# The shared expert's up projections ahead of the routing lists, and its result as the first content of the second sum

## Chip, cores and metric

One NeuronCore of a Trainium2 chip runs the whole kernel. The metric is device microseconds for one execution, median over runs. Engines: TensorE (PE, with its weight loads PEld), VectorE (DVE), ScalarE (ACT), GpSimd (POOL), SyncE (SP, which here only issues DMAs), and 16 DMA engines.

## What is computed

One layer of a decoder trunk over 512 tokens of width 1024: a conditioned norm, three token mixers, a gated residual, then a second conditioned norm and a mixture of experts (64 routed experts of width 256, top 8 of 4 groups; one shared expert), a gated residual and a last norm. The part around the change:

```python
scores = jax.nn.sigmoid(xt @ router_w)          # 512 x 64
...                                             # top 8 experts of each token, weights top_w
yb = (silu(xb @ w1[e]) * (xb @ w3[e])) @ w2[e] * wt    # each expert, on its tokens
routed = sum over experts, scattered to tokens
shared = (silu(xt @ sw1) * (xt @ sw3)) @ sw2    # all 512 tokens
x = x + g2 * (routed + shared)
return rmsnorm(x, final_norm)
```

## The kernel before

Tokens lie in four tiles of 128. The tail of the program, which the change touches, has five stages.

**Projections of the mixers** (from L738 on): weights are split into a high and a low part and multiplied in three passes. On ACT's queue two DMAs of 1 MB (L789) set the DRAM tensor `acc2`, the second of two sums over tokens, to zero from a zeroed tile `z0`; the first sum is `acc`, which gets x after the mixers (L956).

**Output projection and router**, tile by tile (L935 to L985). For each tile `t` the normalised rows `h2` are made on DVE, where POOL supplies the inverse root (`rsq`, L70, stored in `root[t]`); PE transposes them (L968) into `h2F[t]` and multiplies with the router (L973). `route(t)` on DVE finds each token's eight experts (the mask `Mb`, L884). `place(t)` counts positions by PE (L890, L891), then DVE makes eight table indices `ti` and eight rows `row`, one after the other. `fill(t)` has POOL write those eight columns into the DRAM table by eight indirect DMAs (L912): `fill(0)` is issued at tile 2, `fill(1)` and `fill(2)` at tile 3, `fill(3)` after the loop.

**Lists** (L1017 to L1083): from the counts of all tiles (`cps`, L1019) DVE makes `items`, the lists of expert runs, in some sixty small operations; PE turns two of them (L1081). The table is then read back as `idxw` and `idc` (L1098, L1104), and POOL gathers the first run's rows with it (L1120, L1127).

**Shared expert** (L1311 to L1332): for each tile 8 up matmuls in plain f32 (L1319, weights `shw`), silu and product (`act_a`, L1162, L1163), two transposes (L1323), 4 down matmuls (L1330), the gate (L1331) into `ysh[t]`. The scheduler places these instructions wherever an engine has nothing older to do. The results are added to `acc` by four indirect accumulating DMAs (`add_a`, L1191, indices `tok`, L1314).

**Routed experts**: a loop of runs (`pair_of_runs`, 16 of them here, then 9 single blocks). Before it, in an order written out by hand from L1338 on, come the gathers, the transposes of the gathered rows (`x_a`, L1146), copies of the gate row (L1349, L1352) and the splits of the first expert's weights (`split_a(0, u)`, six pieces `wh`, `wl`; ACT makes the high part at L49, DVE the low part at L50). `pair_of_runs` begins on PE with a transpose (L1202) and the up matmuls in three passes (L1153 to L1155).

Each engine takes its instructions in order, so what stands ahead on an engine delays what follows. SP issues the DMAs of expert weights in program order too.

Of the kernel before, what the change touches and what calls it, by code (L numbers as in the profile page):

```python
# [27 lines left out]
E = 64  # L28
# [6 lines left out]
def trunk(ctx, tc, x, c, ada_w, ada_b, norm1, norm2, w_in, conv_a_w, conv_a_b, ln_a_g, ln_a_b,  # L35
# [725 lines left out]
    for j in range(4):  # L761
# [8 lines left out]
        for h in range(2):  # L770
# [10 lines left out]
            for i in range(2):  # L781
                hi, lo = (mT[a][i][:, :, 2 * j + h] for a in range(2))
                A.activation(hi, mt[:, 2 * i:2 * i + 2], AF.Copy, scale=0.5)
                V.scalar_tensor_tensor(lo, mt[:, 2 * i:2 * i + 2], 0.5, hi.bitcast(F32), op0=OP.mult, op1=OP.subtract)
    z0 = mp.tile([P, 4 * E, 2], F32, name="z0")
    G.memset(z0, 0.0)
    a2v = acc2.rearrange("(g p) d -> p g d", p=P)
    for h in range(2):
        nc.scalar.dma_start(a2v[:, :, h * 512:h * 512 + 512],  # L789
                            z0.rearrange("p c x -> p (c x)")[:, None].to_broadcast([P, TT, 512]))  # L790
    tb = mp.tile([P, 4 * E, 2], F32, name="tb")
    G.memset(tb, 0.0)
    tb2 = tb.rearrange("p (c b) x -> p c b x", b=2)
# [142 lines left out]
    for ts in ((0, 1), (2,), (3,)):  # L936
# [7 lines left out]
        for t in ts:  # L944
# [36 lines left out]
                place(0, *sM[0][:2])  # L981
            if t > 1:
                with tc.issue_after(root[t].ins):
                    for v in (0,) if t == 2 else (1, 2):
                        fill(v)  # L985
            if t == 2:
                first_two()
# [26 lines left out]
    load_up(ra, None, 0)  # L1014
    load_down(rad[0], None, 0)

    cps = psh.tile([P, E], F32, name="ps_m", bufs=2)  # L1017
    for t in range(TT):
        T.matmul(cps, ones_b, Mb[:, t], start=(t == 0), stop=(t == TT - 1))  # L1019
# [58 lines left out]
    for a, src in enumerate((v_, c_)):  # L1078
        ips = psh.tile([1, 3, P], F32, name="it_ps", tag="ps_m", bufs=2)
        for j in range(3):  # L1080
            T.matmul(ips[:, j], src[:, j:j + 1], ident, start=True, stop=True)  # L1081
        V.tensor_copy(iv[:, a], ips)
    V.tensor_copy(items[:, 6, 0:2], mi[0:1, 1:3])  # L1083
    hst.close()
    rawst.close()
# [50 lines left out]
    def split_a(j, u, up=None):  # L1136
        if u < 4:
            src = (up or ra[j % 2]).rearrange("p (z k f) -> p k z f", z=2, k=KT)[:, 2 * u:2 * u + 2]
            split(*(w[u].rearrange("p (k z f) -> p k z f", k=2, z=2) for w in (wh, wl)), src)
        else:  # L1140
            split(wh[u], wl[u], rad[j % 2][:, (u - 4) * 1024:(u - 3) * 1024])
# [7 lines left out]
    def up_a(ph, u):  # L1149
        for k in (2 * u, 2 * u + 1):  # L1150
            q = slice(k % 2 * 512, k % 2 * 512 + 512)
            for b in ph:
                T.matmul(ph[b], h2T[0][b][:, k], wh[u][:, q], start=(k == 0), stop=False)  # L1153
                T.matmul(ph[b], h2T[0][b][:, k], wl[u][:, q], start=False, stop=False)  # L1154
                T.matmul(ph[b], h2T[1][b][:, k], wh[u][:, q], start=False, stop=(k == KT - 1))  # L1155

    def ps_up(bs):
        return {b: pse.tile([P, 512], F32, name="ph", bufs=2) for b in bs}

    def act_a(ph, w=None):  # L1160
        hw = ew.tile([P, 256], F32, name="hw", bufs=2)
        A.activation(hw, ph[:, :256], AF.Silu)  # L1162
        V.scalar_tensor_tensor(hw, hw, 1.0 if w is None else w.bitcast(F32), ph[:, 256:], op0=OP.mult, op1=OP.mult)  # L1163
        return hw

    def turn_a(hws):
        n = len(hws)
# [22 lines left out]
    def add_a(y, at, beside=None, to=acc):  # L1190
        st = G.indirect_dma_start(out=to, out_offset=IOA(ap=at, axis=0), in_=y, in_offset=None,  # L1191
                                  compute_op=OP.add, bounds_check=S - 1, oob_is_err=False)
        g = beside or f"run {st.ins.name}"
        if beside:
            tc.declare_no_dep(st.ins, group=g, reason="the rows of a run are distinct")
        tc.add_to_no_dep_group(g, st.ins)
        return g
# [110 lines left out]
        add_a(down_b(i, hT), sa[:, 0, 0:1], to=acc2)  # L1308
        load_down(rad[i % 2], GL, i + 2)

    gs, tok = rad[1][:, :D], ew.tile([P, TT], I32, name="tok")  # L1311
    nc.sync.dma_start(gs, modr[3:4].to_broadcast([P, D]))
    for t in range(TT):
        G.tensor_scalar(tok[:, t:t + 1], iop, 128.0 * t, None, op0=OP.add)  # L1314
    run, ysh = None, []
    for t in range(TT):
        ph = ps_up((t,))[t]
        for k in range(KT):
            T.matmul(ph, h2F[t][:, k], shw[k // 2][:, k % 2 * 512:k % 2 * 512 + 512], start=(k == 0), stop=(k == KT - 1))  # L1319
        hw = act_a(ph)  # L1320
        p3 = pse.tile([P, 2, 2, P], F32, name="p3")
        for k in range(2):
            T.transpose(p3[:, 0, k], hw[:, k * P:(k + 1) * P], ident)  # L1323
        hb = ew.tile([P, 2, P], F32, name="hb", tag="hh")
        A.activation(hb, p3[:, 0], AF.Copy)
        y = rc[1][:, t % 2 * D:t % 2 * D + D] if t > 1 else ew.tile([P, D], F32, name="y", bufs=2)
        for h in range(2):
            py, q = pse.tile([P, 512], F32, name="py", bufs=2), slice(h * 512, h * 512 + 512)
            for k in range(2):
                T.matmul(py, hb[:, k], shw[4 + k][:, q], start=(k == 0), stop=(k == 1))  # L1330
            V.tensor_tensor(y[:, q], py, gs[:, q], op=OP.mult)  # L1331
        ysh.append(y)  # L1332
    wh = [ew1.tile([P, 1024], F32R, name=f"wh{u}") for u in range(6)]
# [4 lines left out]
    with tc.manual_schedule():  # L1338
        gather_a(GA, 0)
        copied = gather_c(GC, 0)  # L1340
        for t in range(2):
            run = add_a(ysh[t], tok[:, t:t + 1], run)
        load_up(rc, GC, 0, copied)
        load_down(rcd, GC, 0)
        for g in range(4):
            x_a(g // 2, g % 2)
        gather_a(GA, 1)
        nc.sync.dma_start(fn[0:1], final_norm[None, :])
        A.activation(gm2, gs, AF.Copy)  # L1349
        for z in range(2):  # L1350
            zq = slice(z * CH, z * CH + CH)
            A.activation(gm2c[zq], gs[zq, z * 512:z * 512 + 512], AF.Copy)  # L1352
        for t in range(2, TT):
            run = add_a(ysh[t], tok[:, t:t + 1], run)
        for u in range(6):
            split_a(0, u)
        load_down(rad[1], GA, 1)
        with ExitStack() as nest:
            for i in range(15):
# [57 lines left out]
```

## Time and profile before

| | |
|---|---|
| time, median of 3 runs | 1458.77 us (1456.04 to 1461.76) |
| the profiled execution's own time | 1467.86 us |
| its span, first to last instruction | 1466.1 us |
| PE busy | 1347.5 us (92%) |
| DVE, ACT, POOL busy | 956.0, 620.3, 264.8 us |
| DMA | 289.13 MB, mean 197 GB/s |

The profile page gives busy time per engine and in 40 slices of the span. The views below it list one engine's instructions in order of time with the idle time before each and what ended it (timeline), the sums of such waits (waits), and the busy time of all engines in chosen stretches (windows). A plain f32 matmul stands as two records, so "x12" of L1319 are six matmuls. "PEclk" is the share of TensorE's full clock that was granted.

### The profile page before, as it was taken

The numbers are of one execution on the slowest core, as the hardware profiler recorded it, in microseconds if no ns is written. First come the engines' busy times: TensorE is split into PE (matmuls) and PEld (weight loads), VectorE is DVE, ScalarE is ACT, GpSimd is POOL, SyncE is SP. The second block draws the span as 40 slices with busy tenths as digits, with TensorE's granted clock in tenths as the row PEclk, the third lists the DMA queues.
The fourth block names the chain that finished last, engine by engine and source line by source line (L and its number), as shares of the span: only waits on it lengthen the run. The fifth ranks groups of instructions, "written<-read, shape, count | busy, mean of one in ns | idle before, by whom it ended". The sixth has DMA issues, their size and how long they took to land. (4 is left out here: it accounts for less than half of the span.)

```text
span 1466.1 us, 24089 instructions
## 1 busy us (share of the span) xinstructions
PE 1347.5 (92%) x8982; PEld 968.7 (66%) x8982; DVE 956.0 (65%) x1816; ACT 620.3 (42%) x1019; POOL 264.8 (18%) x255
## 2 busy tenths in 40 slices
PE   4999999999999979998998978999999999997881
PEld 3877777776766756664686635777677777774660
DVE  6865998987777777233455855666656566564664
ACT  4454334427568658220212213434434443443442
POOL 1000000000000000000000354243342524333332
PEclk8999999999999989999999989999999999999996
DMA  9321231232112117759826348999898989966985
GB/s 339 110 58 31 66 89 47 69 125 92 31 59 80 31 51 237 242 185 333 278 74 238 134 154 266 371 341 322 322 313 294 314 301 337 321 219 206 317 285 208
DMA packets 120634, 289.13 MB, mean 197 GB/s; under 512 B 14883, under 2 KB 68397, under 8 KB 109486
## 3 DMA queue, kind: packets, MB, share of 16 engines
q1 hardware_dynamic: 99266, 242.87, 46.2%
q0 software_dynamic: 17904, 36.01, 10.0%
q10 hardware_dynamic: 3324, 8.49, 1.6%
q8 instruction: 75, 1.23, 0.3%
q14 instruction: 65, 0.53, 0.1%
HBM read 260.24 MB, written 46.97 MB: 210 GB/s over the span
## 5 line engine op out<-in xcount | busy, mean ns | idle before, releaser
L53 PE MATMUL ps_in<-hT_hi,w_hi 128*128 128x512 f32 x496 | 203.9, 411 | 2.7 <-ACT hT_hi L49 2.7
L54 PE MATMUL ps_in<-hT_hi,w_lo 128*128 128x512 f32 x496 | 201.5, 406 | 0.3 <-DVE w_lo L50 0.2
L55 PE MATMUL ps_in<-hT_lo,w_hi 128*128 128x512 f32 x496 | 199.9, 406 | 0.0
L50 DVE TENSOR_TENSOR wl<-ra,wh 128x1024 fp32r<-128x1024 f32 x100 | 122.1, 1224 | 115.2 <-ACT wh L49 111.6
L49 ACT ACTIVATE wh<-ra 128x1024 fp32r<-128x1024 f32 x100 | 105.6, 1060 | 127.8 <-PE ph L1155 90.0
L1153 PE MATMUL ph<-wh,mT_hi 128*128 128x512 f32 x328 | 134.5, 410 | 2.3 <-ACT wh L49 2.3
L1154 PE MATMUL ph<-wl,mT_hi 128*128 128x512 f32 x328 | 129.6, 395 | 0.5 <-DVE wl L50 0.5
L1155 PE MATMUL ph<-wh,mT_lo 128*128 128x512 f32 x328 | 129.3, 394 | 0.0
L50 DVE TENSOR_TENSOR w_lo<-w_raw,w_hi 128x1024 fp32r<-128x1024 f32 x76 | 92.5, 1223 | 51.0 <-ACT w_hi L49 50.8
L53 PEld LDWEIGHTS ps_in<-hT_hi,w_hi 128*128 128x128 f32 x496 | 94.6, 191 | 34.3 <-issue 7.6
L1191 POOL DMA_INDIRECT acc<-y,sa x41 | 65.6, 1599 | 272.9 <-DVE hc L1227 238.0
L54 PEld LDWEIGHTS ps_in<-hT_hi,w_lo 128*128 128x128 f32 x496 | 94.4, 190 | 21.7 <-issue 1.7
L55 PEld LDWEIGHTS ps_in<-hT_lo,w_hi 128*128 128x128 f32 x496 | 94.3, 190 | 21.8 <-issue 2.7
L49 ACT ACTIVATE w_hi<-w_raw 128x1024 fp32r<-128x1024 f32 x76 | 79.3, 1052 | 38.8 <-PE ps_p L55 18.3
L594 DVE SCALAR_TENSOR_TENSOR u<-ut,par,u 128x512 f32<-128x512 f32 x120 | 84.2, 747 | 0.6
L70 POOL TENSOR_TENSOR h<-h,mhalf 128x4 f32<-128x4 f32 x8 | 10.5, 1310 | 358.4 <-DVE h L393 358.4
L1153 PEld LDWEIGHTS ph<-wh,mT_hi 128*128 128x128 f32 x328 | 62.7, 191 | 18.2 <-issue 3.4
L1154 PEld LDWEIGHTS ph<-wl,mT_hi 128*128 128x128 f32 x328 | 62.8, 191 | 15.3 <-issue 1.9
L1155 PEld LDWEIGHTS ph<-wh,mT_lo 128*128 128x128 f32 x328 | 62.6, 191 | 13.3
L1187 DVE TENSOR_TENSOR y<-py,rows 128x512 f32<-128x512 f32 x64 | 44.1, 689 | 31.9 <-PE py L1185 25.1
L49 ACT ACTIVATE wh<-rad 128x1024 fp32r<-128x1024 f32 x34 | 34.1, 1050 | 71.8 <-issue 36.1
L1120 POOL DMA_INDIRECT xg<-h2d,ia x45 | 56.3, 1250 | 20.3 <-issue 8.8
(523 smaller groups left out, 2754.5 us busy)
## 6 DMA issues: line engine op xcount, KB each, us to landing
ra<-in_exp_w_dram SPq DMA_DIRECT2D x52, 1024.0 KB
rc<-in_exp_w_dram SPq DMA_DIRECT2D x34, 1024.0 KB
w_raw<-in_w_in_dram SPq DMA_DIRECT2D x31, 1024.0 KB
rad<-in_exp_w_dram SPq DMA_DIRECT2D x27, 1024.0 KB
adar<-in_ada_w_dram SPq DMA_DIRECT2D x32, 512.0 KB
rcd<-in_exp_w_dram SPq DMA_DIRECT2D x16, 1024.0 KB
ada<-in_ada_w_dram SPq DMA_DIRECT2D x8, 1024.0 KB
gd<-sg SPq DMA_DIRECT2D x24, 256.0 KB
```

What stands on the lines that cost most here:

```text
L49: A.activation(hi, src, AF.Copy)
L50: (lo_engine or V).tensor_tensor(lo, src, hi.bitcast(F32), op=OP.subtract)
L53: T.matmul(ps, l[0], r[0], start=first, stop=False)
L54: T.matmul(ps, l[1], r[0], start=False, stop=False)
L55: T.matmul(ps, l[0], r[1], start=False, stop=last)
L594: V.scalar_tensor_tensor(u[:, ct], ut[ct][:, w:w + S], col("caw", w * 4 + ct), u[:, ct], op0=OP.mult, op1=OP.add)
L1120: G.indirect_dma_start(out=xg[b], out_offset=None, in_=h2d, in_offset=IOA(ap=ia[s][:, b, 0:1], axis=0), bounds_check=S - 1, oob_is_err=False)
L1153: T.matmul(ph[b], h2T[0][b][:, k], wh[u][:, q], start=(k == 0), stop=False)
L1154: T.matmul(ph[b], h2T[0][b][:, k], wl[u][:, q], start=False, stop=False)
L1155: T.matmul(ph[b], h2T[1][b][:, k], wh[u][:, q], start=False, stop=(k == KT - 1))
L1187: V.tensor_tensor(y[:, q], py, gate[:, q], op=OP.mult)
L1191: st = G.indirect_dma_start(out=to, out_offset=IOA(ap=at, axis=0), in_=y, in_offset=None, compute_op=OP.add, bounds_check=S - 1, oob_is_er ...
```

## The change

Five edits. The zeroing of `acc2` goes. The shared expert is split: its 32 up matmuls, the silu, the product and the transposes are written before the lists' counts, for all tiles (silu in `sil`, the linear half copied to `lin`, turned into `hb4`); the 16 down matmuls stay where they were. The four results are written to `acc2` by plain DMAs on SP's queue in place of the accumulating ones into `acc`; `tok` goes. `fill(0)` and `fill(1)` are issued together at tile 2, `fill(2)` at tile 3. The first four weight splits are ordered after the lists and after the last turn, ahead of the transposes of the gathered rows, the last two after the second gather, and the copies of the gate row after all six.

```diff
-    z0 = mp.tile([P, 4 * E, 2], F32, name="z0")
-    G.memset(z0, 0.0)
-    a2v = acc2.rearrange("(g p) d -> p g d", p=P)
-    for h in range(2):
-        nc.scalar.dma_start(a2v[:, :, h * 512:h * 512 + 512],
-                            z0.rearrange("p c x -> p (c x)")[:, None].to_broadcast([P, TT, 512]))
...
                 with tc.issue_after(root[t].ins):
-                    for v in (0,) if t == 2 else (1, 2):
+                    for v in (0, 1) if t == 2 else (2,):
                         fill(v)
...
     load_up(ra, None, 0)
     load_down(rad[0], None, 0)
+    hb4 = [ew.tile([P, 2, 2, P], F32, name=f"hb{i}", tag=n) for i, n in enumerate(("hh", "hl"))]
+    sil, lin = (ew.tile([P, TT, 256], F32, name=n, tag="y", bufs=2) for n in ("sil", "lin"))
+
+    def turn_s(t):
+        p3 = pse.tile([P, 2, 2, P], F32, name="p3")
+        for k in range(2):
+            T.transpose(p3[:, 0, k], sil[:, t, k * P:(k + 1) * P], ident)
+        return A.activation(hb4[t // 2][:, t % 2], p3[:, 0], AF.Copy)
+
+    for t in range(TT):
+        ph = ps_up((t,))[t]
+        for k in range(KT):
+            last_up = T.matmul(ph, h2F[t][:, k], shw[k // 2][:, k % 2 * 512:k % 2 * 512 + 512], start=(k == 0), stop=(k == KT - 1))
+        A.activation(sil[:, t], ph[:, :256], AF.Silu)
+        A.activation(lin[:, t], ph[:, 256:], AF.Copy)
+        V.tensor_tensor(sil[:, t], sil[:, t], lin[:, t], op=OP.mult)
+    with tc.issue_after(last_up.ins):
+        for t in range(TT):
+            turned = turn_s(t)
     cps = psh.tile([P, E], F32, name="ps_m", bufs=2)
...
-        V.tensor_copy(iv[:, a], ips)
+        listed = V.tensor_copy(iv[:, a], ips)
...
-    gs, tok = rad[1][:, :D], ew.tile([P, TT], I32, name="tok")
+    gs = rad[1][:, :D]
     nc.sync.dma_start(gs, modr[3:4].to_broadcast([P, D]))
+    ysh = []
     for t in range(TT):
-        G.tensor_scalar(tok[:, t:t + 1], iop, 128.0 * t, None, op0=OP.add)
-    run, ysh = None, []
-    for t in range(TT):
-        ph = ps_up((t,))[t]
-        for k in range(KT):
-            T.matmul(ph, h2F[t][:, k], shw[k // 2][:, k % 2 * 512:k % 2 * 512 + 512], start=(k == 0), stop=(k == KT - 1))
-        hw = act_a(ph)
-        p3 = pse.tile([P, 2, 2, P], F32, name="p3")
-        for k in range(2):
-            T.transpose(p3[:, 0, k], hw[:, k * P:(k + 1) * P], ident)
-        hb = ew.tile([P, 2, P], F32, name="hb", tag="hh")
-        A.activation(hb, p3[:, 0], AF.Copy)
         y = rc[1][:, t % 2 * D:t % 2 * D + D] if t > 1 else ew.tile([P, D], F32, name="y", bufs=2)
...
-                T.matmul(py, hb[:, k], shw[4 + k][:, q], start=(k == 0), stop=(k == 1))
+                T.matmul(py, hb4[t // 2][:, t % 2, k], shw[4 + k][:, q], start=(k == 0), stop=(k == 1))
...
         copied = gather_c(GC, 0)
-        for t in range(2):
-            run = add_a(ysh[t], tok[:, t:t + 1], run)
+        with tc.issue_after(listed.ins), tc.issue_after(turned.ins):
+            for u in range(4):
+                split_a(0, u)
         load_up(rc, GC, 0, copied)
         load_down(rcd, GC, 0)
         for g in range(4):
             x_a(g // 2, g % 2)
         gather_a(GA, 1)
+        for t in range(TT):
+            nc.sync.dma_start(acc2[t * P:(t + 1) * P], ysh[t])
         nc.sync.dma_start(fn[0:1], final_norm[None, :])
+        for u in range(4, 6):
+            split_a(0, u)
         A.activation(gm2, gs, AF.Copy)
...
-        for t in range(2, TT):
-            run = add_a(ysh[t], tok[:, t:t + 1], run)
-        for u in range(6):
-            split_a(0, u)
```

How the built instructions move, at three places.

PE, from the shared expert's first matmuls to the positions of tile 3 (`ps_m<-Mb,before`, for `place(3)`), before; `h2F` ends in 7109 to 7112 for tiles 0 to 3, `shw` in 7103 to 7106 for the pieces of the up weights; `p` is the transpose of the silu product.

```order
L1319 MATMUL ph<-shw_7106,h2F_7109 128x512
L973 MATMUL plg<-rw,h2F_7112 128x64 x4
L1019 MATMUL ps_m<-Mb,ones_b 128x64
L890 MATMUL ps_m<-Mb,ones_b 128x64
L1319 MATMUL ph<-shw_7103,h2F_7110 128x512 x2
L1319 MATMUL ph<-shw_7104,h2F_7110 128x512 x2
L1323 MATMUL p_7975<-ident,hw 128x128 x2
L1319 MATMUL ph<-shw_7105,h2F_7110 128x512
L891 MATMUL ps_m<-Mb,before 128x64
L1330 MATMUL py<-shw_7107,hb 128x512
```

The same stretch now; `h2F` ends in 7105 to 7108, `shw` in 7099 to 7102, and `sil` is the product. Rows of tiles 1 to 3 that read alike are left out.

```order
L1033 MATMUL ph<-shw_7102,h2F_7105 128x512
L967 MATMUL plg<-rw,h2F_7108 128x64 x4
L1033 MATMUL ph<-shw_7099,h2F_7106 128x512 x2
L1033 MATMUL ph<-shw_7099,h2F_7107 128x512 x2
L1033 MATMUL ph<-shw_7099,h2F_7108 128x512 x2
L1033 MATMUL ph<-shw_7102,h2F_7108 128x512 x2
L1027 MATMUL p_7823<-ident,sil 128x128 x2
L1042 MATMUL ps_m<-Mb,ones_b 128x64
L885 MATMUL ps_m<-Mb,before 128x64
L1027 MATMUL p_7827<-ident,sil 128x128 x2
L1333 MATMUL py<-shw_7103,hb_7771 128x512
```

The counts and the positions of tile 3 stood behind 13 of the 32 up matmuls; now they stand behind all 32 and the first turn.

POOL, from the inverse roots of tiles 0 to 2 (`ss`) to the first gather's list entry, before:

```order
L70 TENSOR_TENSOR ss_7123<-ss_7123,mhalf 128x1 x3
L912 DMA table<-row,ti 32768x2 x8
L1314 TENSOR_SCALAR tok<-iop 128x1 x4
L70 TENSOR_TENSOR ss_7123<-ss_7123,mhalf 128x1
L912 DMA table<-row,ti 32768x2 x24
L1117 TENSOR_LOAD items
```

and now:

```order
L70 TENSOR_TENSOR ss_7119<-ss_7119,mhalf 128x1 x3
L906 DMA table<-row,ti 32768x2 x16
L70 TENSOR_TENSOR ss_7119<-ss_7119,mhalf 128x1
L906 DMA table<-row,ti 32768x2 x16
L1140 TENSOR_LOAD items
```

The inverse root of tile 3 stood behind 8 table writes; now it stands behind 16.

ACT, from the last router score to the loop, before; `hw` is silu, `hb` the turned product, `rows` the gate row:

```order
L863 ACTIVATE score<-plg 128x64
L1162 ACT_TABLE_LOAD
L1162 ACTIVATE hw<-ph 128x256
L1325 ACTIVATE hb<-p_7975 128x256
L49 ACTIVATE mT_hi_5782<-pt 128x512 x2
L1325 ACTIVATE hb<-p_8052 128x256
L1349 ACTIVATE rows_8077<-rad_7753 128x1024
L49 ACTIVATE wh_8065<-ra_7750 128x1024
L49 ACTIVATE wh_8070<-rad_7752 128x1024
L1204 ACTIVATE xct<-pt 128x512
```

and now:

```order
L857 ACTIVATE score<-plg 128x64
L1034 ACT_TABLE_LOAD
L1034 ACTIVATE sil<-ph 128x256
L1035 ACTIVATE lin<-ph 128x256
L1028 ACTIVATE hb_7772<-p_7835 128x256
L49 ACTIVATE wh_8056<-ra_7746 128x1024
L49 ACTIVATE wh_8059<-ra_7746 128x1024
L49 ACTIVATE mT_hi_5782<-pt 128x512 x4
L49 ACTIVATE wh_8061<-rad_7748 128x1024
L1357 ACTIVATE rows_8068<-rad_7749 128x1024
L1218 ACTIVATE xct<-pt 128x512
```

Four of the six high parts of the first expert's weights now stand ahead of the gathered rows' splits (`mT_hi`), and the gate row's copies behind all of them.

## Rows read from the trace of the kernel before

**Rows 1.** The profile page: the span and busy time by engine.

```profile
span 1466.1 us, 24089 instructions
PE 1347.5 (92%) x8982; PEld 968.7 (66%) x8982; DVE 956.0 (65%) x1816; ACT 620.3 (42%) x1019; POOL 264.8 (18%) x255
```

**Rows 2.** Windows from the router's last tile to the loop: stretch, length, busy time of PE, PEld, DVE, ACT, POOL with their instructions, granted clock, DMA share, GB/s.

```profile
840.00:860.00 20.00, 11.69 (x53) 6.16 (x51) 8.97 (x60) 3.09 (x5) 14.26 (x15) 0.93 0.53 189
860.00:880.00 20.00, 18.27 (x49) 8.22 (x50) 15.36 (x88) 1.15 (x3) 10.05 (x10) 0.81 0.29 105
880.00:900.00 20.00, 19.41 (x55) 9.01 (x54) 7.79 (x15) 2.53 (x6) 8.55 (x10) 1.00 0.75 230
900.00:920.00 20.00, 16.22 (x63) 12.36 (x62) 12.86 (x15) 13.00 (x16) 7.21 (x5) 0.83 1.03 334
940.00:960.00 20.00, 20.00 (x113) 13.93 (x112) 12.33 (x18) 8.99 (x13) 4.65 (x6) 1.00 0.98 345
```

**Rows 3.** Waits from 846 to 866 us, of DVE and PE: engine, line, what was waited for, us in total, times, longest. Then the first silu in ACT's timeline (start, length, ..., idle time before), and one queue of the DMA view from 850 to 855 us: packets, MB, share of 16 engines.

```profile
DVE jk L907 <- remote: 3.1, 1, 3.1
DVE jk L907 <- DVE gt L872: 1.2, 1, 1.2
DVE gt L872 <- issue: 1.1, 1, 1.1
PE p L1323 <- DVE hw L1163: 7.5, 1, 7.5
857.21 0.38 ACT L1162 ACTIVATE hw<-ph 128x256 f32<-128x256 f32 x1 [6.31 <-issue]
q14 instruction: 1, 0.01, 0.4%
```

**Rows 4.** PE's timeline in the shared expert: start, length, line, operation, tile, form, count, idle time before.

```profile
836.09 6.25 PE L1319 MATMUL ph<-shw,h2F 128*128 128x512 f32 x10 [2.38 <-DVE tm L951]
842.18 0.60 PE L968 MATMUL ps_t<-ident,h 128*128 128x128 f32 x4
845.90 1.00 PE L973 MATMUL plg<-rw,h2F 128*128 128x64 f32 x8
864.15 0.23 PE L891 MATMUL ps_m<-Mb,before 128*128 128x64 bf16 x1
869.48 5.31 PE L1319 MATMUL ph<-shw,h2F 128*128 128x512 f32 x12
894.70 1.04 PE L1146 MATMUL pt<-ident,xg 128*128 128x128 f32 x8
896.76 3.70 PE L1330 MATMUL py<-shw,hb 128*128 128x512 f32 x8 [0.53 <-ACT hb L1325]
900.30 1.04 PE L1146 MATMUL pt<-ident,xg 128*128 128x128 f32 x8
902.36 0.63 PE L1202 MATMUL pt<-ident,xc 128*128 128x128 f32 x4 [1.02 <-issue]
905.24 0.78 PE L1153 MATMUL ph<-wh,mT_hi 128*128 128x512 f32 x1 [2.26 <-ACT wh L49]
```

**Rows 5.** POOL's timeline: the table writes (L912), the inverse root of tile 3 (L70) and the first gathers (L1120, L1127).

```profile
827.58 1.48 POOL L912 DMA_INDIRECT table<-row,ti  x1 [0.30 <-issue]
833.18 0.96 POOL L912 DMA_INDIRECT table<-row,ti  x1 [0.30 <-DVE gtop L867]
839.57 0.57 POOL L70 TENSOR_TENSOR ss<-ss,mhalf 128x1 f32<-128x1 f32 x1 [3.35 <-DVE ss L960]
868.00 0.96 POOL L912 DMA_INDIRECT table<-row,ti  x1 [5.66 <-issue]
877.31 0.95 POOL L912 DMA_INDIRECT table<-row,ti  x1 [0.30 <-issue]
884.40 1.09 POOL L1120 DMA_INDIRECT xg<-h2d,ia  x1 [0.61 <-DMA idc<-table]
887.74 1.05 POOL L1127 DMA_INDIRECT xc<-h2d,ic  x1 [0.27 <-POOL ic L1126]
```

**Rows 6.** DVE's timeline: two large operations of the router tiles (L954, L964), the mask of tile 3 (L884), its table indices (L905), the lists' last copy (L1082).

```profile
828.28 1.07 DVE L954 TENSOR_TENSOR h<-x,sc 128x512 f32<-128x512 f32 x1
840.17 0.75 DVE L964 SCALAR_TENSOR_TENSOR h<-h,ss,sh 128x512 f32<-128x512 f32 x1 [0.49 <-POOL ss L70]
863.87 0.20 DVE L884 CAST Mb<-M 128x64 bf16<-128x64 f32 x1
866.92 0.14 DVE L905 TENSOR_SCALAR ti<-d 128x8 int32<-128x8 f32 x1
879.59 1.01 DVE L1082 CAST items<-it_ps 1x384 int32<-1x384 f32 x2 [1.27 <-PE it_ps L1081]
```

**Rows 7.** The zeroing and what runs beside it: its two DMAs in ACT's timeline, two windows (columns as in rows 2), and waits from 655 to 700 us.

```profile
661.26 0.96 ACTq L789 DMA_DIRECT2D acc<-z  x2
665.00:670.00 5.00, 4.46 (x19) 2.33 (x17) 0.00 (x0) 0.00 (x0) 0.00 (x0) 1.00 1.03 401
670.00:675.00 5.00, 3.48 (x16) 2.11 (x16) 0.81 (x2) 0.00 (x0) 0.00 (x0) 1.00 1.06 399
PE ps_a L721 <- DMA adar<-in_ada_w_dram: 3.1, 4, 1.5
PE ps_p L53 <- ACT w_hi L49: 2.3, 1, 2.3
```

More of the change, by code (lines that the diff above doesn't have):

```diff
@@ L1015, in trunk, with ps_up, act_a @@
     load_down(rad[0], None, 0)
+    def ps_up(bs):
+        return {b: pse.tile([P, 512], F32, name="ph", bufs=2) for b in bs}
+    def act_a(ph, w=None):
+        hw = ew.tile([P, 256], F32, name="hw", bufs=2)
+        A.activation(hw, ph[:, :256], AF.Silu)
+        V.scalar_tensor_tensor(hw, hw, 1.0 if w is None else w.bitcast(F32), ph[:, 256:], op0=OP.mult, op1=OP.mult)
+        return hw
+    hb4 = [ew.tile([P, 2, 2, P], F32, name=f"hb{i}", tag=n) for i, n in enumerate(("hh", "hl"))]
[15 more added lines that the diff above has]
+            turned = turn_s(t)
     cps = psh.tile([P, E], F32, name="ps_m", bufs=2)
@@ L1155, in up_a @@
                 T.matmul(ph[b], h2T[1][b][:, k], wh[u][:, q], start=False, stop=(k == KT - 1))
[L1157 to L1164, printed above, removed]
     def turn_a(hws):
```

## The prediction

> **What bounds the kernel now.** I read the page first: PE is busy 92% of a span of 1466.1 us, no other engine over 65% [rows 1]. So a change counts where PE idles, or where something late makes it idle. The windows show the two kinds of stretch [rows 2]. In the loop (940 to 960) PE works 20.00 of 20 us at full clock: whatever moves the loop's first matmul (905.24 [rows 4]) passes unchanged to the end. In the tail of the router it does not fill its time: 11.69 of 20 us from 840 to 860, then 18.27 at a granted clock of 0.81, that is half speed for part of it.
>
> The waits name the hole: PE stands 7.5 us for a silu product [rows 3]. Its first silu starts at 857.21 after ACT has stood 6.31 us for nothing that the profile shows; in the same time DVE has waits of 3.1 us ("remote") and 1.1 us (issue), and a code packet (q14) passes [rows 3]. I call these together the stall. DVE's mask of tile 3 comes at 863.87 [rows 6], its positions on PE at 864.15 [rows 4], the first table index at 866.92 [rows 6], the first write of tile 3 at 868.00, the eighth ends at 877.31 + 0.95 = 878.26, the first gather is at 884.40, the last at 887.74 [rows 5]. Behind these PE turns gathered rows at 894.70, 900.30 and 902.36, and then waits 2.26 us for a weight split [rows 4].
>
> The sum is made against the profiled execution, 1467.86 us by its own time: 9.1 above the median of the runs, 1458.77. A measurement of this kernel can tell about 0.5% from no change: 7.3 us, so 1451.5 and 1466.1 are the limits.
>
> **The change part by part.** *Table writes.* The inverse root of tile 3 ran at 839.57, after eight writes that end at 833.18 + 0.96 = 834.14 [rows 5]. Now eight more stand ahead. A write and the gap before it take 0.95 + 0.30 [rows 5], 1.26 in round figures, so 10.1 us, to 844.2. A write beside DVE's 1.07 us product at 828.28 took 1.48 instead of 0.96 [rows 5, 6]; two such meetings add 1.0: the root starts at 845.3, the normalising of tile 3 at 845.9 instead of 840.17 (+5.7), and ends 0.75 later [rows 6], at 846.7. Bounds: 0 for the meetings, or the larger operation's length each time (2.1). The Trainium skill, page "SBUF — State Buffer", section "Who interferes with whom", says that a DVE operation with two SBUF inputs and a GpSimd one that reads SBUF exclude each other for the whole instruction. The row shows half of one operation (0.52 of 1.07), not the whole; by the page's rule the root would start up to 1.1 us later than here.
>
> *Up matmuls ahead of the lists.* PE has five of them, 6.25 us from 836.09, ahead of the transposes of tile 3 (842.18 before [rows 4]). These now wait until 846.7, some 4.4 us that PE has no use for. Then 27 ups, at 5.31 / 6 = 0.885 each [rows 4], make 23.9; transposes, router products, counts, positions and first turn, 2.8 (0.60 + 1.00 + 0.2 to 0.3 for each small group [rows 4]); half clock after the wait, as in the five ups that took 6.25 instead of 4.4, costs between 0 and 1.8, I take 1.0. So tile 3's positions come at 846.7 + 27.7 = 874.4 if nothing interrupts PE (864.15 before).
>
> *The interruption.* Silu needs its table loaded after the last router score. Everything behind tile 3's transposes moves by 4.5, so the first silu moves from 857.21 to 861.7 if ACT's stall recurs, and both reads of the first `ph` (two operations of 0.38 [rows 3]) end at 862.5. PE reaches tile 2's ups, which need that buffer, after 11 ups and 2 us of router work: 846.7 + 9.7 + 2.0 = 858.4 to 859. It waits 3.5, and with some half clock I take 3.9. Bounds: 0 (no stall) and 7.5 [rows 3]. I take 3.9, since the wait has its place in the program, right behind the table load, and nothing in the change removes that. DVE's part of the stall costs nothing: the mask would come at 863.87 + 4.5 = 868.4, under the ups, and has 6 us of cover.
>
> *From the positions to the loop.* First write after 868.00 − 864.15 = 3.85, and 0.35 (my estimate, half of one of 0.75) for a product in DVE's way: with positions at 878.3, at 882.5. Eight writes 10.26, to the first gather 6.14 [rows 5]: 898.9. DVE's side is no later: the lists' copy ended 879.59 + 1.01 = 880.60 [rows 6], 16.45 behind the positions, the gather 3.8 behind that, together 898.6. Gathers 4.39 (884.40 to 887.74 + 1.05 [rows 5]); landing between 0 and 5.9 (888.79 to 894.70, where PE was busy with other things till then [rows 4, 5]), I take 3.6; the last transposes 1.02 + 0.63 [rows 4]. The loop begins at 908.5, against 905.24: **+3.3**. The downs, the other turns and x's two turns lie ahead of it in the time of writes and gathers: 16 × 0.925 (3.70 for four [rows 4]) is 14.8 of the 24 us there.
>
> *Weight splits, gate row copies.* The first four splits move under that same time, where ACT is idle; PE's 2.26 us wait for them [rows 4] goes, but what is late next is the gathered rows, so nothing is gained beyond the sum above. If the lists were early, they would be on the path again.
>
> *Plain writes.* Four writes of 512 KB on SP's queue replace four accumulating DMAs of as many bytes; POOL loses them and `tok`. The stretch 900 to 920 moves 334 GB/s at DMA share 1.03 [rows 2] either way. Behind the writes SP issues the loop's later weights; PE's 2.26 us for a split, not for a load, is the nearest wait. I take 0, bounds −1 and +2.
>
> *Zeroing.* Its two DMAs leave ACT's queue at 661.26; from 665 to 675 the share is 1.03 to 1.06 and PE idles for `adar`, 3.1 us in four waits, and once 2.3 for a split, some 15 us later [rows 7]. Three of the four `adar` waits, 2.7 us, lie in or shortly behind that traffic. Bounds: 0 and 6.7 (all of both, and 1.3 of half clock behind the second, an estimate below the 1.8 that it cost the five ups). I take **−2.7**: the same 4 MB less to move, but only what the load itself had lost.
>
> Sum: 1467.86 + 3.3 − 2.7 = 1468.5. The remaining 9.1 between this profile and the median I take as it is, if the stall belongs to every run: 1459.4.
>
> The Trainium skill, page "Runtime: NRT & Kernel Launch", section "The ~15µs preamble/postamble breakdown", says that a profile's total exceeds the reported time by about 6.2 us whatever the kernel. Here the span alone is already 7.3 above the median, so the trace does not agree that it lies around the program.
>
> **The rivals.** *ACT does not wait.* If its 6.31 us go with the new order, the 3.9 are gone: 1455.5. For it: table load and code packet may pass earlier, beside the ups. Against it: the wait's place.
>
> *The stall is only in the profiled execution* (the other side, slower). For it: the 9.1 us are nearly what PE lost there, 7.5 of idle time and part of the half clock. Then the ordinary runs before have no hole to fill; their lists come early, and the change moves these behind 19 more ups. The changed kernel's own chain has no stall either: 1467.86 − 0.6 − 2.7 = 1464.6 for every run, +5.8. It decides from the point where the positions of tile 3 fall later than the stall left them; each us more, in a PE wait or in the gathers, counts in full, and 1.5 suffice for over 0.5%. Against it: a stall with a place and a code packet would recur.
>
> *The zeroing costs more.* With no interruption and all 6.7: 1451.5.
>
> *The change does less than it says*: if downs and turns did not fit ahead of the gathers the ups' early place would only push the lists; that is inside the second rival.
>
> **How the numbers follow.** Forecast 0.38, no ACT wait 0.20, stall only in the profile 0.27, zeroing 0.15. Faster by over 0.5%: 0.12 of the last and 0.07 of the second, with the landing at its low end: 0.19. Slower: 0.15 of the third, and 0.04 of the forecast with the wait at 7.5 and the meetings at their bound: 0.19. The rest is 0.62. The range reaches from under the zeroing's case, 1450, to 1468, the third with 3 us more; about one in ten lies beyond each end.
>
> **What would show it.** In the new profile: the root of tile 3 near 845, a PE wait of 4 us ahead of its transposes, another of 3 to 4 ahead of tile 2's ups behind ACT, positions of tile 3 near 878, its first table write near 882, the first gather near 899, the loop near 908, all earlier by the 2 to 3 us of the zeroing. No ACT wait and positions by 872 mean the second case; the same with a median above 1464 means the third. I am wrong as a whole if positions come before 866, if the loop waits for weights or splits, or if the writes to `acc2` hold up SP's loads.

## The result: 0.9% slower, and how the new profile reads

The changed kernel takes 1472.76 us (median of 8 runs, 1466.08 to 1476.97) against 1459.36 for the kernel before in runs beside it (1454.74 to 1464.45); the ratio is 1.0092 (95% interval 1.0071 to 1.0112). The profiled execution took 1471.06 with a span of 1469.2. It is slower, outside the forecast range of 1450 to 1468.

PE's timeline of the changed kernel, in the stretch of [rows 4]:

```profile
833.76 4.56 PE L1033 MATMUL ph<-shw,h2F 128*128 128x512 f32 x10 [0.86 <-DVE tm L945]
845.53 1.12 PE L962 MATMUL ps_t<-ident,h 128*128 128x128 f32 x4 [7.21 <-DVE h L958]
846.43 1.92 PE L1033 MATMUL ph<-shw,h2F 128*128 128x512 f32 x2
851.63 21.68 PE L1033 MATMUL ph<-shw,h2F 128*128 128x512 f32 x50
873.56 0.19 PE L885 MATMUL ps_m<-Mb,before 128*128 128x64 bf16 x1
906.20 1.09 PE L1216 MATMUL pt<-ident,xc 128*128 128x128 f32 x4 [4.00 <-DVE wl L50]
906.94 0.78 PE L1176 MATMUL ph<-wh,mT_hi 128*128 128x512 f32 x1
```

PE waits 7.21 us for the rows of tile 3. After two more ups among the router's products it runs 25 ups without a gap (x50 are 25 matmuls), and only then multiplies for tile 3's positions. POOL's timeline shows what held these rows up and what follows the positions, answering to [rows 5]; ACT's shows the first silu, answering to [rows 3]:

```profile
827.02 1.48 POOL L906 DMA_INDIRECT table<-row,ti  x1 [0.30 <-DVE tm L945]
835.17 1.33 POOL L906 DMA_INDIRECT table<-row,ti  x1 [0.30 <-DVE gt L869]
...
843.13 0.96 POOL L906 DMA_INDIRECT table<-row,ti  x1 [0.30 <-issue]
844.11 0.57 POOL L70 TENSOR_TENSOR ss<-ss,mhalf 128x1 f32<-128x1 f32 x1
877.19 1.01 POOL L906 DMA_INDIRECT table<-row,ti  x1 [13.70 <-issue]
886.09 0.96 POOL L906 DMA_INDIRECT table<-row,ti  x1 [0.30 <-DVE it L1088]
893.41 1.09 POOL L1143 DMA_INDIRECT xg<-h2d,ia  x1 [0.61 <-DMA idc<-table]
894.56 1.56 POOL L1130 TENSOR_SCALAR idc<-idc,up 128x256 int32<-128x256 int32 x1
897.35 1.25 POOL L1149 COPY ic<-idc 128x2 int32 x1
898.86 1.04 POOL L1150 DMA_INDIRECT xc<-h2d,ic  x1 [0.27 <-POOL ic L1149]
852.07 1.28 ACT L1034 ACT_TABLE_LOAD   x1
853.36 0.38 ACT L1034 ACTIVATE sil<-ph 128x256 f32<-128x256 f32 x1
```

The root of tile 3 stands right behind the sixteenth table write. After the writes of tile 2 POOL is idle for 13.70 us ahead of tile 3's writes: it waits for positions. ACT's first silu follows its table load at once; the 6.31 us of [rows 3] are not there. The waits of DVE in [rows 3] ("remote", issue) have no counterpart either: the stall that the forecast built on does not occur in this execution.

The page, answering to [rows 1], PE's waits for `adar` from 655 to 700 us, answering to [rows 7], and 80 us around the stretch as a window (columns as in [rows 2]):

```profile
PE 1348.5 (92%) x8982; PEld 969.3 (66%) x8982; DVE 954.5 (65%) x1816; ACT 621.3 (42%) x1023; POOL 257.4 (18%) x246
PE ps_a L721 <- DMA adar<-in_ada_w_dram: 0.8, 2, 0.6
830.00:910.00 80.00, 60.07 (x192) 31.01 (x191) 47.66 (x220) 18.13 (x32) 36.85 (x39) 0.89 0.41 151
```

PE's busy time is nearly the same, 1348.5 against 1347.5 us. The loss is waiting, and most of it stands in this one window: PE is idle for 19.9 of its 80 us, against 9.8 in the second profile of the kernel before that the next section shows.

### The profile page after: what moved, and what is told of

Same layout as the page of the kernel before. It is cut to its first block, busy times and chain, and to the rows that moved or that the text cites. A ratio compares the mean times of both kernels' runs of the same rounds, so it can differ in the third digit from the quotient of the medians.

```text
span 1469.2 us, 24089 instructions
## 1 busy us (share of the span) xinstructions
PE 1348.5 (92%) x8982; PEld 969.3 (66%) x8982; DVE 954.5 (65%) x1816; ACT 621.3 (42%) x1023; POOL 257.4 (18%) x246
## 3 DMA queue, kind: packets, MB, share of 16 engines
HBM read 260.24 MB, written 44.88 MB: 208 GB/s over the span
## 5 line engine op out<-in xcount | busy, mean ns | idle before, releaser
L53 PE MATMUL ps_in<-hT_hi,w_hi 128*128 128x512 f32 x496 | 203.7, 411 | 2.7 <-ACT hT_hi L49 2.7
L55 PE MATMUL ps_in<-hT_lo,w_hi 128*128 128x512 f32 x496 | 199.6, 405 | 0.0
L53 PEld LDWEIGHTS ps_in<-hT_hi,w_hi 128*128 128x128 f32 x496 | 94.5, 191 | 34.9 <-issue 8.7
L55 PEld LDWEIGHTS ps_in<-hT_lo,w_hi 128*128 128x128 f32 x496 | 94.3, 190 | 21.7 <-issue 2.7
L70 POOL TENSOR_TENSOR h<-h,mhalf 128x4 f32<-128x4 f32 x8 | 10.5, 1310 | 359.6 <-DVE h L393 359.6
```

The costliest lines, as they stand in the source:

```text
L53: T.matmul(ps, l[0], r[0], start=first, stop=False)
L55: T.matmul(ps, l[0], r[1], start=False, stop=last)
```

## Experiments

The runs fell on four chips, A to D, each used once; the chip of the two rows with a dash is not known. Runs of one chip share their runs of the kernel before. For each trace the table gives what counts: us from the end of the last output projection to the positions of tile 3, to the first gather and to the loop's first matmul, each taken from PE's and POOL's timeline. "(stall)" marks traces in which DVE waits for a releaser that the profile calls "remote", 1.2 us or more at a time, somewhere between 828 and 873 us; the others have no such wait there. A trace is one execution, and executions of one kernel differ by some us, so a difference of 1 or 2 us between two traces alone shows nothing.

| kernel | chip | positions | gather | loop | ratio to before (95%) |
|---|---|---|---|---|---|
| before, as forecast from (stall) | – | 30.4 | 50.7 | 71.5 | |
| before, second profile | A | 16.1 | 42.0 | 62.0 | 1.0005 (0.9982–1.0027) |
| changed, as above | – | 40.7 | 60.5 | 74.0 | 1.0092 (1.0071–1.0112) |
| lists first | A | 26.9 | 48.5 | 67.0 | 1.0013 (0.9990–1.0036) |
| writes as before | A | 32.3 | 52.2 | 66.9 | 1.0011 (0.9989–1.0032) |
| changed + zeroing | A | 43.0 | 64.4 | 78.0 | 1.0133 (1.0106–1.0159) |
| lists first, writes as before (stall) | B | 23.2 | 48.4 | 70.6 | 0.9966 (0.9942–0.9991) |
| the same, splits late too (stall) | B | 30.4 | 50.5 | 74.3 | 1.0005 (0.9982–1.0029) |
| the same + zeroing (stall) | B | 24.7 | 49.5 | 75.0 | 1.0014 (0.9986–1.0041) |
| before + moved writes (stall) | B | 24.4 | 54.9 | 76.7 | 1.0036 (1.0007–1.0065) |
| changed, again (stall) | C | 41.7 | 61.7 | 77.3 | 1.0002 (0.9982–1.0022) |
| lists first, writes as before (stall) | C | 30.4 | 50.9 | 73.4 | 0.9969 (0.9947–0.9991) |
| before + moved writes (stall) | C | 25.3 | 55.6 | 77.4 | 1.0013 (0.9989–1.0037) |
| mixture (stall) | C | 23.5 | 50.5 | 69.9 | 0.9967 (0.9948–0.9987) |
| before + moved writes | D | 25.6 | 48.0 | 66.7 | 1.0068 (1.0032–1.0105) |
| mixture | D | 16.2 | 40.8 | 57.7 | 0.9948 (0.9932–0.9963) |
| changed, third time | D | 43.0 | 64.5 | 77.0 | 1.0090 (1.0066–1.0114) |

**Is the stall in every run?** The kernel before, unchanged.

> The kernel before, unchanged, profiled a second time. Theory (the stall of 851 to 864 us was in the one profiled execution alone, and the changed kernel's positions of tile 3, behind 19 more up matmuls, are what costs 13 us): no PE wait of 7.5 us ahead of the first turn, ACT's first silu right behind its table load near 851, positions of tile 3 near 855 instead of 864.15, first gather near 875, the loop's first matmul near 896, own time 1457 to 1461. Rival (the stall belongs to every run, and the loss is made later, by splits and stores): the same waits of 7.5 and 6.3 us, positions near 864, loop near 905, own time near 1467 with a profile and 1459 without.

PE, ACT and POOL of this trace, and the window around the stretch:

```profile
834.34 4.56 PE L1319 MATMUL ph<-shw,h2F 128*128 128x512 f32 x10 [0.83 <-DVE tm L951]
839.22 0.66 PE L968 MATMUL ps_t<-ident,h 128*128 128x128 f32 x4 [0.32 <-DVE h L964]
848.46 0.38 PE L1323 MATMUL p<-ident,hw 128*128 128x128 f32 x2
849.64 0.19 PE L891 MATMUL ps_m<-Mb,before 128*128 128x64 bf16 x1
874.41 0.44 PE L1323 MATMUL p<-ident,hw 128*128 128x128 f32 x2 [3.33 <-DVE hw L1163]
895.51 0.80 PE L1153 MATMUL ph<-wh,mT_hi 128*128 128x512 f32 x1 [2.26 <-ACT wh L49]
844.27 1.28 ACT L1162 ACT_TABLE_LOAD   x1
845.57 0.39 ACT L1162 ACTIVATE hw<-ph 128x256 f32<-128x256 f32 x1
859.50 0.96 POOL L912 DMA_INDIRECT table<-row,ti  x1 [0.30 <-issue]
875.46 1.09 POOL L1120 DMA_INDIRECT xg<-h2d,ia  x1 [0.61 <-POOL ia L1118]
830.00:910.00 80.00, 70.18 (x237) 38.60 (x236) 51.95 (x226) 20.48 (x32) 44.03 (x48) 0.94 0.67 223
```

No wait of 7.5, silu right behind the table load, positions at 849.64 instead of 864.15, the loop at 895.51 instead of 905.24, and its own time 1457.57 instead of 1467.86. Of the 10.3 us between the two executions 9.5 lie between the last output projection and the loop (71.5 against 62.0): this accounts for the 9.1 us between [rows 1]'s execution and the median. Part of it stands ahead of the place that the prediction named: PE's wait of 2.38 us and the five ups of 6.25 [rows 4] are 0.83 and 4.56 here. Note a second thing: POOL writes tile 3's first column only at 859.50, 10 us behind the positions, since it is still busy with 24 earlier ones. In this kernel positions have 10 us of slack on POOL, and the gathers, ready before PE has done the shared expert, have some more on PE.

**Lists ahead of the ups again.** The `for t in range(TT)` block with the ups and turns moves behind the lists:

```diff
-    for t in range(TT):
-        ph = ps_up((t,))[t]
...
     cps = psh.tile([P, E], F32, name="ps_m", bufs=2)
...
+    for t in range(TT):
+        ph = ps_up((t,))[t]
...
     gs = rad[1][:, :D]
```

> The changed kernel, with the up matmuls, silu, product and turns written behind the lists again; plain stores, table writes, splits and the missing zeroing as changed. Theory: positions of tile 3 return to near 858 (from 873.6), the first gather moves from 893.4 to near 880, the loop's first matmul from 906.9 to 897 to 900, and the time falls by 8 to 10 us, to 1463 to 1465. Rival (splits and stores): less than 3 us, 1470 or more.

**Table writes as before.**

```diff
-                    for v in (0, 1) if t == 2 else (2,):
+                    for v in (0,) if t == 2 else (1, 2):
```

> The changed kernel, with the table writes of tile 0 issued at tile 2 and those of tiles 1 and 2 at tile 3 again; all else as changed. Theory: the inverse root of tile 3 moves from 844.1 to near 839, PE's wait of 7.2 us ahead of tile 3's transposes falls to 2 to 3, all that follows up to the gathers comes 4.5 us earlier: 1468. Rival (PE has slack later, or POOL's moved writes fall on the path): within 1.5 us of the changed kernel, 1472.

Each takes the time back to that of the kernel before, within the intervals: 1.0013 and 1.0011. In the stretch itself both stay 5 us above its 62.0; what makes up for it lies outside, the missing zeroing (below, some 3 us) among it. Rows of the first, then of the second:

```profile
845.63 1.11 PE L962 MATMUL ps_t<-ident,h 128*128 128x128 f32 x4 [6.96 <-DVE h L958]
860.13 0.19 PE L885 MATMUL ps_m<-Mb,before 128*128 128x64 bf16 x1
866.65 0.96 POOL L906 DMA_INDIRECT table<-row,ti  x1 [0.30 <-issue]
```

```profile
835.57 0.65 PE L962 MATMUL ps_t<-ident,h 128*128 128x128 f32 x4 [0.30 <-DVE h L958]
862.11 0.19 PE L885 MATMUL ps_m<-Mb,before 128*128 128x64 bf16 x1
865.74 1.01 POOL L906 DMA_INDIRECT table<-row,ti  x1 [10.31 <-issue]
```

With lists first PE still waits 6.96 for tile 3, but POOL is busy until the positions' writes start (0.30). With the writes back there is no such wait, and POOL idles 10.31 for the positions. The table shows how slack eats a delay. Writes back (with the rest of the change), against the kernel before: +16.2 at the positions, +10.2 at the gather, +4.9 at the loop. The changed kernel, against writes back: +8.4, +8.3, +7.1. The new order of the ups has used up the slack, and the moved writes pass nearly unchanged to the end. My expectations, 4.5 us for the writes and 8 to 10 for the lists, were both too low: the medians fell by 12.6 and 12.5, to 1460.19 and 1460.28.

**The writes alone.** The same line changed in the kernel before, on three chips.

> The kernel before with the table writes of tiles 0 and 1 together, a third time. Without the stall (kernel before near 1460): theory (moved writes alone keep PE waiting 5 to 7 us ahead of tile 3's transposes, but later waits of PE shrink by part of it): ratio 1.002 to 1.004, loop 64 to 66 us behind the last output projection instead of 62.0; rival (harmless alone): 1.000, 62 to 63. With the stall (near 1470): 1.001 to 1.004 as in the two runs so far.

Without the stall 1.0068, loop 66.7 us behind the projection instead of 62.0. So the moved writes are not harmless alone. Whether they cost more than the 1.002 to 1.004 that I expected is open, since the interval begins at 1.0032; the profiled execution, 1458.43, is the fastest of its six, so its 66.7 is rather low. The two runs beside a stall,

> The kernel before with one edit of the change alone: the table writes of tiles 0 and 1 together at tile 2. Theory (the writes alone cost a part): root of tile 3 near 844, PE's wait ahead of tile 3's transposes 7 us, 65 to 68 us from the last output projection to the loop, 1463 to 1466. Rival (they cost only where the lists stand behind all ups): 62, 1460.

> The kernel before with the table writes of tiles 0 and 1 together, once more. On a chip without the stall: root of tile 3 near 844 instead of 837.8, PE's wait ahead of its transposes 5 to 7 us; theory, half of that reaches the loop: ratio 1.002 to 1.004; rival (all of it or more): 1.006. With the stall: 1.0036 as measured.

gave 1.0036 and 1.0013. That less of it shows there is likely but not shown, since the intervals overlap.

**Both undone, and the splits.** Lists first and writes as before, with early splits; then with

```diff
-        with tc.issue_after(listed.ins), tc.issue_after(turned.ins):
-            for u in range(4):
-                split_a(0, u)
...
         A.activation(gm2, gs, AF.Copy)
...
+        for u in range(6):
+            split_a(0, u)
```

> The changed kernel with both undone: lists ahead of the later up matmuls, and table writes grouped as before; plain stores, early splits and the missing zeroing stay. From the last output projection to the loop the runs so far took 62.0 us (kernel before, second profile), 67.0 (lists first), 66.9 (writes regrouped), 74.1 (changed kernel). Theory (moved order and moved writes use up the same slack of PE, 5 us each alone and more together; the zeroing was worth 2 to 4): 60 to 62, so 1456 to 1458, faster than before. Rival (the 5 us that both single undoings kept come from splits or stores): 66 to 67, 1460.

> As the run before, and the six weight splits back behind the transposes of the gathered rows too, the gate row's copies ahead of them; left of the change are the plain stores, the missing zeroing and the silu in two reads. Theory: 62 us from the last output projection to the loop, with a wait for the first split of 2 us, 1457 to 1459, at most 2 us behind the run before. Rival (early splits cost, since DVE does them beside the shared expert's products): 2 us or more faster than the run before.

> Lists first, writes as before, early splits, plain stores, no zeroing, once more. On a chip without the stall: theory 60 to 63 us from the last output projection to the loop, ratio to the kernel before 0.996 to 0.998; rival (the late turns and downs, all behind the last up matmul, keep PE from filling its waits): 65 or more and 1.000. With the stall: 0.9966 as measured.

With early splits 0.9966 and 0.9969, with late ones 1.0005 on the same chip as the first: the early splits are worth some 0.4% (the two intervals against the kernel before just overlap, but the runs of the two kernels, twelve each, differ by 6.1 us, give or take 3.0), and the rival (they cost) fell. The way over the stretch, 70.6 and 73.4, was longer than expected; chips B and C put the stall into these traces.

**Zeroing and plain stores.**

> The changed kernel with the two 1 MB DMAs that set the second sum to zero put back (their result is then overwritten by the plain stores): the price of the zeroing alone. Prediction's term: 2.7 us slower, 1475.5, with waits for adar of some 3 us at 667 to 693; its bounds 0 and 6.7. Rival (the loads only shift against each other): 0 to 1 us.

> The same kernel as the second of this call, with the zeroing put back: against it, the price of the zeroing; against the kernel before, that of the plain stores in place of accumulating ones. Theory: 2 to 4 us slower than without zeroing, and within 1.5 us of the kernel before, 1460. Rival (the stores hold up later weight loads): 1462 or more, with waits for loads in the loop.

The zeroing put back costs 0.0041 in ratio on top of the changed kernel, 0.0009 in the other pair; the intervals overlap in both, so neither size is settled by the times. The traces settle it better. From the end of the input projections (L55, tile `ps_in`) to the first output projection (L53, `ps_o`), a way that holds the zeroing and lies ahead of every other edit and of the stall, it takes 116.3 to 120.4 us with zeroing (seven traces) and 113.7 to 116.0 without (ten), 2.9 less on average. PE's waits for `adar` there come to 1.9 to 4.2 us with zeroing and to 0.5 to 1.2 without; for the changed kernel with zeroing,

```profile
PE ps_a L721 <- DMA adar<-in_ada_w_dram: 1.9, 2, 1.4
```

to be read against its 0.8 without. The stores alone are within the measurement of the kernel before, as expected; no wait for loads appeared.

**The changed kernel on a chip with the stall.**

> The changed kernel, unchanged, beside the kernel before. The four runs with lists first, writes regrouped and neither on the second chip all showed a DVE stall of 6 to 10 us in the router, and there the kernel before took 1470.7; on the first chip none did, and it took 1460. If the kernel before takes about 1470 here (stall in its runs), theory (the changed order hides the stall under the up matmuls, but not its own 8 us of waiting): 1473 to 1476, ratio 1.001 to 1.004. If it takes 1460: 1473, ratio 1.009. Rival (the changed kernel carries the stall on top): ratio 1.009 on either chip.

1.0002: where the kernel before takes 1470.48, the changed one takes 1469.04, no more than elsewhere. But not for the reason that I gave. DVE's and PE's rows of that trace, and the turn of `xc`:

```profile
832.87 0.17 DVE L862 TENSOR_TENSOR gs<-gtop 128x8 f32<-128x8 f32 x1
839.86 0.69 DVE L945 TENSOR_TENSOR tm<-ps_o,g 128x512 f32<-128x512 f32 x1 [6.82 <-remote]
840.61 7.34 PE L1033 MATMUL ph<-shw,h2F 128*128 128x512 f32 x10 [8.06 <-DVE tm L945]
847.79 0.60 PE L962 MATMUL ps_t<-ident,h 128*128 128x128 f32 x4
874.28 0.19 PE L885 MATMUL ps_m<-Mb,before 128*128 128x64 bf16 x1
909.11 1.09 PE L1216 MATMUL pt<-ident,xc 128*128 128x128 f32 x4 [3.39 <-DMA xc<-h2d,ic]
```

The stall sits earlier, in the making of tile 3's rows: 6.82 us on DVE, 8.06 on PE. It runs beside POOL's moved writes, which hold up the same rows; PE no longer waits ahead of the transposes, and positions come 41.7 us behind the projection against 40.7. Two delays of one thing in parallel cost once. ACT has no wait between table load and first silu here either. The third time, without a stall, is

> The changed kernel beside the kernel before, a third time. Without the stall: 1.009 as in the first measurement; with it: 1.000 to 1.002. Rival (the ratio does not depend on the chip, and the run with 1.0002 was chance): 1.004 to 1.009 with the stall.

1.0090: the ratio differs between chips, as the theory had it. Since each chip was used once, chip and session cannot be told apart.

**A mixture that beats both.** The kernel before without zeroing, with plain stores, and with

```diff
+        with tc.issue_after(listed.ins):
+            for u in range(4):
+                split_a(0, u)
...
+        for t in range(TT):
+            nc.sync.dma_start(acc2[t * P:(t + 1) * P], ysh[t])
         nc.sync.dma_start(fn[0:1], final_norm[None, :])
+        for u in range(4, 6):
+            split_a(0, u)
```

> The kernel before with three edits alone: no zeroing, results stored plainly to the second sum, and the first four weight splits right behind the lists' last copy (the last two ahead of the gate row's copies). Order of up matmuls, turns, downs and table writes as before. Theory (zeroing 2 to 4, early splits the wait of 2.3 ahead of the loop and up to 5.6): ratio 0.994 to 0.997. Rival (splits on DVE delay the shared expert's products, stores hold up weight loads): 0.998 to 1.001.

> No zeroing, plain stores, early splits, all else as in the kernel before, a second time. Without the stall: theory (the gain does not hang on the stall): 0.995 to 0.998. Rival (the early splits fill time that only the stall makes): 0.999 or more. With the stall: 0.997 as measured.

0.9967 beside the stall and 0.9948 without: 1451.94 against 1459.84. Its PE enters the loop thus, to be read against the 2.26 us of wait and the 0.80 us of the first matmul in the second profile of before:

```profile
886.50 0.63 PE L1196 MATMUL pt<-ident,xc 128*128 128x128 f32 x4 [1.02 <-issue]
886.88 0.48 PE L1147 MATMUL ph<-wh,mT_hi 128*128 128x512 f32 x1
```

No wait for a split, and a granted clock of 1.00 from 884 to 887. Of the 4.3 us by which the stretch is shorter (57.7 against 62.0) 2.5 stand here. Another 4.3 us lie ahead of the stretch, 3.2 of them ahead even of the zeroing's place, where the two kernels are alike, and 2.7 behind it. This execution, 1446.41, is 5.5 below its kernel's median, so these parts add up to more than the 7.9 between the medians.

## Why the prediction was wrong, step by step

**The step that failed is the baseline:** "the remaining 9.1 between this profile and the median I take as it is, if the stall belongs to every run". It does not. On chips A and D no trace has it (seven traces), on B and C all eight have it, and the runs of the kernel before take about 1460 on A and D and 1470 to 1471 on B and C. The runs of the first measurement, median 1459.36, lie with A and D, and the changed kernel's trace has no stall. [rows 1]'s own time, 1467.86, lies above all 48 runs of the kernel before that the ratios of the first measurement and of A and D rest on (at most 1464.45), and amid those of B and C (1462.36 to 1480.34). So profile and median look like two kinds of chip, though the chip of that profile is not known. The forecast's mechanism (idle time that the ups fill) thus had nothing to fill, and the second rival ("the stall is only in the profiled execution", 0.27, 1464.6) is what happened: positions fall behind the ups, and each us counts. I held against it that a stall with a place in the program would recur. It does, on B and C, but not where the medians were measured; and I gave less weight to what spoke for the rival, that 9.1 us is nearly 7.5 plus some half clock. That nearness was the evidence.

**The size, 13.4 instead of 5.8.** Against the sum for that case, 1467.86 − 0.6 − 2.7 = 1464.6, the profiled execution took 1471.06, 6.5 more, and the median 1.7 more still. The 6.5 are 1.9 ahead of the end of the last output projection, nothing from there to the positions, 0.8 less from there to the first gather, 3.9 more from it to the loop, and 1.4 behind.
- *Root of tile 3:* forecast 845.3, measured 844.11. Two of the sixteen writes took 1.48 and 1.33 us instead of 0.96. The prediction laid this to DVE's product (`h<-x,sc`); the rows show the sum ahead of it:

```profile
826.99 0.69 DVE L946 TENSOR_TENSOR x<-x,tm 128x512 f32<-128x512 f32 x1
834.98 0.69 DVE L946 TENSOR_TENSOR x<-x,tm 128x512 f32<-128x512 f32 x1
```

  The writes start at 827.02 and 835.17, while the sum has 0.66 and 0.50 us to go, and take 0.52 and 0.37 longer, nearly as much. The Trainium skill, page "SBUF — State Buffer", section "Who interferes with whom", has a DVE operation with two SBUF inputs and a GpSimd one that reads SBUF exclude each other, so that the later one waits until the first is through; the trace agrees with it, and the prediction's "half of one operation (0.52 of 1.07), not the whole" was read against the wrong operation.
- *PE's wait for tile 3:* forecast 4.4, measured 7.21. I took five ups from 836.09 on, and 6.25 us for them, from an execution with the stall, where PE had a granted clock of 0.73 from 836 to 842.4, half speed for part of it, after a wait of 2.38 [rows 4]. Here they began at 833.76 after a wait of 0.86 and took 4.56 at a granted clock of 1.00, so PE was done 4.0 earlier and waited longer. The end of the wait was right (846.7, measured 845.53).
- *Positions:* forecast 874.4 less 2.7 for the zeroing, so 871.7; measured 873.56. The difference of 1.9 came in ahead of the stretch: the last output projection ended at 832.89, 0.8 earlier than before and not 2.7. The zeroing is not to blame: the way that holds it was 2.4 us shorter (115.6 against 118.0, counted as in the experiment), but the input projections ahead of it, which the change leaves alone, ended at 658.92 instead of 656.07 (652.5 to 658.9 in the seventeen traces).
- *ACT's interruption* (3.9): absent. Named as its test, it was seen at once in the new profile. It is absent on chip C too, so even where the stall is in the runs the reason given ("the wait has its place in the program, right behind the table load") did not hold.
- *Positions to first gather:* forecast 20.6, measured 19.85.
- *Gather to loop:* forecast 9.6, measured 13.5. Two terms were mis-sized. The first is the gathers: 4.39 forecast, 6.49 measured (893.41 to 898.86 + 1.04). POOL's two operations between them took 1.56 and 1.25 us; in the kernel before, and in DVE's rows of the changed one beside them, stand

```profile
885.55 0.50 POOL L1107 TENSOR_SCALAR idc<-idc,up 128x256 int32<-128x256 int32 x1
887.27 0.20 POOL L1126 COPY ic<-idc 128x2 int32 x1
893.50 2.34 DVE L50 TENSOR_TENSOR wl<-ra,wh 128x1024 fp32r<-128x1024 f32 x2
897.34 1.22 DVE L50 TENSOR_TENSOR wl<-ra,wh 128x1024 fp32r<-128x1024 f32 x1
```

  The early weight splits run on DVE just there. In the eight traces in which a split runs beside the gathers these take 5.2 to 8.3 us, in the nine without one 4.4. The second term is the landing, 3.6 behind the end of the last gather's issue: it was 6.3. The view of the tile `xc` gives it from the start of the issue:

```profile
DMA to landing us min/median/max: 7.2/7.3/7.4
```

  898.86 + 7.3 is 906.2, when PE turns `xc`. The "4.00 <-DVE wl" beside that row is the last to end by the profile, but PE's turn reads only `xc`; the same kernel on chip C has "3.39 <-DMA xc" in this place. My upper end, 5.9, was read off the wrong row: at 894.70 [rows 4] PE turns `xg`, and `xc`, issued last, only at 902.36. In the second profile of before `xc` lands 8.4 us after its issue and is turned at 892.63, 5.4 us later, so there the landing costs nothing. The last transposes took 0.74 instead of 1.65.
- *Loop to end:* 562.2 us against 560.8, 1.4 that no term covers; the seventeen traces take 557.6 to 564.0.
- *Zeroing:* −2.7, within 0 to 6.7; 2.9 by the traces. The "4 MB less to move" beside it were 2.1: the page has 46.97 MB written to HBM before and 44.88 after.
- *Splits:* costed at nothing, since "what is late next is the gathered rows". PE's wait for a split is gone in the changed kernel, but the splits' DVE half makes the gathered rows 2.1 us later. Where the lists are early they are worth 0.4%, as the sentence behind it said.

The chain's order (writes, root, tile 3, ups, positions, writes, gathers, loop) was right at every link, and "I am wrong as a whole if positions come before 866" did not occur. The harm was done where a sum from one execution was set against a median from others; the gathers and the landing added 3.9 to it.

## What to carry to other kernels

Where the profiled execution lies above the median of the runs, find the place of the difference in its trace before any of its idle time is counted as room: here 9.1 us of "idle PE" belonged to a profile with a stall that the measured runs did not have. A delay is eaten by slack at every engine that it passes (16.2, 10.2, 4.9); two edits that use the same slack must be costed together, and the second one pays in full. A landing is bounded only by the row that uses that very tile. Work moved into another engine's idle time can slow a third one beside it: look at what runs next to POOL's gathers before DVE work is moved there.

## What the hardware showed that I had not expected

The same kernel takes 1459.4 to 1460.1 us on some chips and 1470.5 to 1470.7 on others, and the traces of the latter have waits in the router that those of the former lack. They are not of DVE alone, nor in one place. DVE waits for "remote" 1.2 to 6.8 us at a time, around 828 to 840 in all eight and again between 854 and 873 in six; POOL for 0.5 to 2.3; ACT 5.0 us ahead of a router score in three traces, and 6.8 to 10.3 us ahead of a silu in five. [rows 3]'s trace has the same pattern. What makes it is open: code packets pass at like places in both kinds (a q14 packet at 850.0 in the second profile of before and at 854.8 in the one with the stall), so these do not tell them apart. Nor is it shown that the waits alone make the 10 to 11 us between the two kinds of run; between the two profiles of the kernel before 9.5 of 10.3 us lie in this stretch.
